# A sliding-window copy kernel: one more staged batch, larger packets, direct copies in long strided DMAs, fewer semaphore updates

## The chip, the cores and the metric

The kernel runs on one core of a Trainium2 chip. The metric is the device time in microseconds (us) of one execution; medians of several runs are quoted. Ratios are computed as the mean time of one kernel's fast runs over the mean time of the other's fast runs of the same rounds, so they are not quite the ratio of the quoted medians.

"KB" is 1024 bytes and "GB" is 10^9 bytes. A *block* is 32 KB, half a window of one batch. A DMA is cut into *packets*; the trace records start, duration, queue and size of each packet, but not which of the 16 DMA engines moved it.

## The reference

```python
batch, length, dim = (32, 4096, 256)       # float32
window_size, stride = 64, 32
n_windows = (length - window_size) // stride + 1        # 127
result = np.zeros((batch, n_windows, window_size, dim), dtype=np.float32)
for i in range(n_windows):
    start = i * stride
    result[:, i] = x[:, start:start + window_size].copy()
```

This is pure copying. A batch has 128 blocks of input. Window i consists of blocks i and i+1, so a batch has 254 blocks of output: nearly every input block is written twice.

## The kernel before

There are two ways to make the output, and the kernel uses both at once:

- *Direct* batches go from memory to memory: 254 blocks through the DMA engines, each of them both read from and written to memory (HBM).
- *Staged* batches are loaded into SBUF (128 blocks, read once) and stored from there twice, as first halves and as second halves. A store always takes all 128 rows, so it moves 256 blocks. The two surplus blocks fall on a neighbour's window and are overwritten later by an "edge" copy, which waits for the store. A staged batch costs the engines 384 blocks, but it reads memory for 128 of them only.

So staging costs DMA bytes and saves memory traffic: of the 220.95 MB that the profile below counts as read from memory, 174.8 are direct (edges included) and 46.1 loaded; of the 267.09 MB written, the same 174.8 are direct and 92.3 stored.

Three queues are used: SP issues direct copies (q1 in the profile), ACT issues loads and stores (q10), GpSimd issues the edges (q0) near the end.

```python
DIRECT, IN, OUT = 32768, 16384, 16384        # packet sizes in bytes

    def windows(self, q, b, w0, n, half=None, piece=DIRECT):
        blk = self.blk
        row = [1, 2 * blk if half is None else blk]
        h = half or 0
        return q.dma_start(
            out=self.oap((b * self.nw + w0) * 2 + h, [[2 * blk, n], row]),
            in_=self.xap(b * self.nb + w0 + h, [[blk, n], row]),
            max_dma_last_dim=piece,          # a longer row is cut into pieces of this size
        )
# ... cut ...
    staged = [*range(1, B, 3)]               # 11 of 32 batches
# ... cut ...
    edges = [(b, 0 if b - 1 in staged else 112, 15) for b in direct[:-1]]    # 15 windows each
# ... cut: a direct copy is 16 whole windows (32 packets + 16 semaphore packets),
#     or two copies of 16 half windows, more of the latter while the staged queue loads ...
        ring_r.wait_ge(near, 16)             # the edges start when the direct copies are nearly over
        for b, w, n in edges:
            for k in (b - 1, b + 1):
                if k in place and b != last:
                    st.wait_stored(ring_r, place[k])
            count(c.windows(ring_r, b, w, n), rest)
```

## Time and profile before

The median is 754.37 us of 6 runs (752.63 to 756.47).

The page of the profile, kernel before: the span; the DMA busy share and the GB/s in 40 equal slices; all packets; the direct queue q1 and the staged queue q10 with packets, MB and share of the 16 engines' span; memory traffic.

```profile
span 749.4 us, 322 instructions
...
DMA  8999999999999999999999999999999999999996
GB/s 360 401 427 429 427 429 428 434 423 418 420 424 423 418 424 415 422 427 427 414 427 417 429 432 429 430 422 430 429 423 421 423 421 419 425 426 423 431 409 262
DMA packets 18290, 313.26 MB, mean 418 GB/s; under 512 B 4336, under 2 KB 4336, under 8 KB 4528
...
q1 hardware_dynamic: 8016, 154.32, 48.8%
q10 hardware_dynamic: 9104, 138.41, 44.0%
...
HBM read 220.95 MB, written 267.09 MB: 651 GB/s over the span
...
```

The engines are 0.9 busy or more in every slice but the first and the last, so there is no gap to close. The time is bytes times the time of a packet, plus a start and an end. The packet records of the same trace, with the sum of each queue's packet times divided by 16 engines:

| kernel before | packets | size | mean ns | commonest ns | sum / 16, us |
|---|---|---|---|---|---|
| q1, direct | 4704 | 32 KB | 1236 | 1213 | 363.3 |
| q10, staged | 8448 | 16 KB | 624 | 611 | 329.6 |
| q0, edges | 608 | 32 KB | 1248 | 1213 | 47.4 |
| semaphore packets | 4336 | 4 B | 9 | 9 | 2.4 |

All packets of the three queues sum to 744.6 us. If every packet took the commonest time of its size (1213, 611, and for other sizes in the same way), the sum would be 729.5 us; I call that the *floor* and the rest, 15.1 us, the *excess*. 32 KB in 1213 ns on 16 engines is 432 GB/s.

### The profile page before, as it was taken

How to read it: one execution, taken by the hardware profiler on the slowest of the kernel's cores; microseconds unless marked ns; L12 is line 12 of the kernel's file. 1: busy time of each engine (PE TensorE's matmuls, PEld its weight loads, DVE VectorE, ACT ScalarE, POOL GpSimd, SP SyncE). 2: the span in 40 equal slices, each digit the busy share in tenths (PEclk: the TensorE clock that was granted, in tenths of full speed). 3: DMA queues.
4: the chain of work that ended last, by engine and by line, in shares of the span. 5: the costliest groups of instructions: out<-in, count | busy, mean ns of one | idle time of the engine just before them, and what ended most of it. 6: DMA issues, size and time to landing. Idle time of an engine off the chain costs nothing.

```text
span 749.4 us, 322 instructions
## 1 busy us (share of the span) xinstructions
POOL 12.8 (2%) x26
## 2 busy tenths in 40 slices
POOL 0000000000000000000000000000000000040100
DMA  8999999999999999999999999999999999999996
GB/s 360 401 427 429 427 429 428 434 423 418 420 424 423 418 424 415 422 427 427 414 427 417 429 432 429 430 422 430 429 423 421 423 421 419 425 426 423 431 409 262
DMA packets 18290, 313.26 MB, mean 418 GB/s; under 512 B 4336, under 2 KB 4336, under 8 KB 4528
## 3 DMA queue, kind: packets, MB, share of 16 engines
q1 hardware_dynamic: 8016, 154.32, 48.8%
q10 hardware_dynamic: 9104, 138.41, 44.0%
q0 software_dynamic: 1168, 20.51, 6.5%
q14 instruction: 2, 0.02, 0.0%
HBM read 220.95 MB, written 267.09 MB: 651 GB/s over the span
## 4 chain that ended last, share of the span: by engine, by line
another core or an unknown queue 92%; POOL 2%; issue 0%; POOLq 0%; SPq 0%
POOL out_dram L34 2%; POOL out_dram L44 0%; POOLq L236 0%; SPq L172 0%; POOLq L114 0%
## 5 line engine op out<-in xcount | busy, mean ns | idle before, releaser
L34 POOL DMA_DIRECT2D out_dram<-in_x_dram x21 | 12.0, 576 | 691.3 <-DMA out_dram<-in_x_dram 654.0
L44 POOL DMA_DIRECT2D out_dram<-in_x_dram x1 | 0.6, 581 | 0.0
L222 POOL MEMSET const-float32-0.0<- 128x1 f32 x1 | 0.1, 98 | 0.2 <-issue 0.2
L222 POOL MEMSET const-bfloat16-1.0<- 128x1 bf16 x1 | 0.1, 101 | 0.0
L222 POOL MEMSET const-float32-1.0<- 128x1 f32 x1 | 0.1, 98 | 0.0
L222 POOL MEMSET const-uint8-127<- 128x1 uint8 x1 | 0.1, 98 | 0.0
## 6 DMA issues: line engine op xcount, KB each, us to landing
out_dram<-in_x_dram SPq DMA_DIRECT2D x92, 1024.0 KB, 100.7
out_dram<-xb ACTq DMA_DIRECT2D x21, 4096.0 KB, 139.7
out_dram<-in_x_dram SPq DMA_DIRECT2D x110, 512.0 KB, 90.3
xb<-in_x_dram ACTq DMA_DIRECT2D x10, 4096.0 KB, 131.4
out_dram<-in_x_dram POOLq DMA_DIRECT2D x20, 960.0 KB, 38.5
xb<-in_x_dram ACTq DMA_DIRECT2D x4, 1024.0 KB, 15.7
out_dram<-xb ACTq DMA_DIRECT2D x2, 1024.0 KB, 113.4
out_dram<-xb ACTq DMA_DIRECT2D x4, 512.0 KB, 96.9
```

What stands on the lines that cost most here:

```text
L34: return q.dma_start(out=self.oap((b * self.nw + w0) * 2 + h, [[2 * blk, n], row]), in_=self.xap(b * self.nb + w0 + h, [[blk, n], row]), m ...
L44: return q.dma_start(out=self.oap((b * self.nw + w0) * 2, [[part, 16], [2 * self.blk, n], row]), in_=self.xap(b * self.nb + w0, [[part, 16 ...
L222: nc = _bacc.Bacc("TRN2", target_bir_lowering=False, num_devices=1)
```

## The change

Its intent, as the diff shows it: 12 staged batches in place of 11; 32 KB packets for loads and stores, 64 KB for edges; direct copies always half windows, 112 packets in one DMA in a pattern of 16 neighbouring rows by 7; few DMAs and so few semaphore packets (16 for each DMA of q1 and q10: 3264 for 204 DMAs on q1 before); staged loads and stores in interleaved parts (every second or fourth row), meant, I take it, to give both big queues like shares of the turns.

```diff
-DIRECT, IN, OUT = 32768, 16384, 16384
+DIRECT, IN, OUT, REST = 32768, 32768, 32768, 65536
+    def many(self, q, b, w0, n, half):
+        return q.dma_start(
+            out=self.oap((b * self.nw + w0) * 2 + half, [[2 * self.blk, 16], [32 * self.blk, n], [1, self.blk]]),
+            in_=self.xap(b * self.nb + w0 + half, [[self.blk, 16], [16 * self.blk, n], [1, self.blk]]),
+        )
 ... loads: one DMA of 128 rows -> two of 64 interleaved rows (four for the first batch);
     stores: each half in two such parts, or four for second halves of odd batches ...
-    staged = [*range(1, B, 3)]
+    staged = [0, 3, 6, 9, 11, 14, 17, 20, 22, 25, 28, 31]
 ... batch 0 may now be staged; a direct batch between two staged ones gets edges of 8 and 7 windows ...
-        for i, (b, w) in enumerate(sixteens):
-            ... cut: whole or half windows by a running share ...
+        for i, (b, w, n, half) in enumerate(main):
+            count(c.many(ring_d, b, w, n, half), near if i == len(main) - 1 else done)
 ...
-            count(c.windows(ring_r, b, w, n), rest)
+            count(c.windows(ring_r, b, w, n, None, REST), rest)
```

More of the change, by code (lines that the diff above doesn't have):

```diff
@@ L87, in load, with split @@
         i = g % len(self.tiles)
-        b, c, n = self.items[g]
         if self.count[self.stored[i]]:
             q.wait_ge(self.stored[i], self.count[self.stored[i]])
-        step = 128 // n
-        parts = [(k, 4, 32, 1) for k in range(4)] if g == 0 else [(0, step, n, step)]
-        for rows in parts:
-            self.issue(self.c.load(q, self.tiles[i], b, c, rows), self.loaded[i])
+        for rows in self.split(4 if g == 0 else 2):
+            self.issue(self.c.load(q, self.tiles[i], *self.items[g], rows), self.loaded[i])
         self.after_load[g] = self.count[self.loaded[i]]
+    def split(self, parts):
+        return [(k, parts, 128 // parts, 1) for k in range(parts)]
     def store(self, q, g):
         i = g % len(self.tiles)
-        b, c, n = self.items[g]
         q.wait_ge(self.loaded[i], self.after_load[g])
-        step = 128 // n
-        parts, end = [((0, step, n, step), 0), ((0, step, n, step), 1)], []
+        parts = [(rows, half) for half in (0, 1) for rows in self.split((2, 4 if g % 2 else 2)[half])]
+        end = []
         if g == len(self.items) - 1:
-            parts = [((0, 1, 128, 1), 1), ((0, 1, 32, 1), 0)]
+            parts = [(rows, 1) for rows in self.split((2, 4 if g % 2 else 2)[1])] + [((0, 1, 32, 1), 0)]
             end = [(96, 1, 32, 1)] + [(32 + k, 4, 16, 1) for k in range(4)]
         for rows, half in parts:
-            self.issue(self.c.store(q, self.tiles[i], b, c, rows, half), self.stored[i])
+            self.issue(self.c.store(q, self.tiles[i], *self.items[g], rows, half), self.stored[i])
         for rows in end:
-            self.issue(self.c.store(q, self.tiles[i], b, c, rows, 0), self.ended)
+            self.issue(self.c.store(q, self.tiles[i], *self.items[g], rows, 0), self.ended)
         self.after_store[g] = self.count[self.stored[i]]
@@ L140 @@
     c = Copier(x, out, B, L, D, W, S, n_win)
-    staged = [*range(1, B, 3)]
-    items = [(b, -1 if b == B - 1 else 0, c.nb) for b in staged]
-    place = {b: g for g, (b, _, n) in enumerate(items) if n == c.nb}
+    staged = [0, 3, 6, 9, 11, 14, 17, 20, 22, 25, 28, 31]
+    items = [(b, 1 if b == 0 else -1 if b == B - 1 else 0) for b in staged]
+    place = {b: g for g, b in enumerate(staged)}
     direct = [b for b in range(B) if b not in staged]
@@ L157, in count @@
         total[sem] += 16
-    sixteens = []
+    main, edges, singles = [], [], [(B - 1, c.nw - 1, 1)]
+    if 0 in staged:
+        singles.append((0, 0, 0))
+    last = B - 2
     for b in direct:
-        w = 15 if b - 1 in staged else 0
-        sixteens += [(b, w + 16 * j) for j in range((c.nw - w) // 16)]
-    singles = [(B - 1, c.nw - 1, 1)]
-    edges = [(b, 0 if b - 1 in staged else 112, 15) for b in direct[:-1]]
-    last = B - 2
-    edges.append((last, 112, 4))
-    first_loads, loads, stores = 6 * 17, 5 * 17, 6 * 34
-    turns = share = 0
+        before, behind = b - 1 in staged, b + 1 in staged
+        w = 15 if before and (not behind or b == last) else 8 if before else 0
+        if b == last:
+            w = 0
+        main += [(b, w + 16 * j, min(7, 7 - j), half) for j in range(0, 7, 7) for half in (0, 1)]
+        if b == last:
+            edges.append((b, 112, 4))
+        elif before and behind:
+            edges += [(b, 0, 8), (b, 120, 7)]
+        else:
+            edges.append((b, 0 if before else 112, 15))
     with tc.tile_critical():
         st.run(ring_s)
-        for i, (b, w) in enumerate(sixteens):
-            sem = near if i == len(sixteens) - 2 else done
-            second = turns - first_loads - stores
-            loading = turns < first_loads or 0 <= second < loads
-            share += 120 if turns < 16 or -8 <= second < 16 else 90 if loading else 18
-            if share >= 120:
-                share -= 120
-                turns += 4
-                count(c.windows(ring_d, b, w, 16, 0), done)
-                count(c.windows(ring_d, b, w, 16, 1), sem)
-            else:
-                turns += 3
-                count(c.windows(ring_d, b, w, 16), sem)
-            if i == len(sixteens) // 2:
+        for i, (b, w, n, half) in enumerate(main):
+            count(c.many(ring_d, b, w, n, half), near if i == len(main) - 1 else done)
+            if i == len(main) // 2:
                 for b, w, half in singles:
```

## The prediction

> **What bounds it now.** The 16 DMA engines. The page's slices show DMA 0.9 busy from the second to the last but one; no other engine matters. The trace's packet records, summed and divided by 16: queue q1 (direct copies) 4704 packets of 32 KB, mean 1236 ns, 363 us; q10 (staged) 8448 of 16 KB, 624 ns, 330 us; q0 (edges) 608 of 32 KB, 1248 ns, 47 us; 4336 semaphore packets of 9 ns, 2.4 us; the rest 2 us. That is 744.8 us of the 749.4 us span: no gap to close but some 6 us before the first packet and a ragged tail of some 3 us. Time = bytes x ns per packet.
>
> The commonest packet takes 1213 ns for 32 KB, 611 ns for 16 KB: 432 and 429 GB/s over 16 engines. [...] only 2% of excess over the floor is left.
>
> Where the excess sits: while the staged queue loads (about 60-150 and 440-530 us) 32 KB packets take 1213-1218 ns; while it stores, 1240-1260. In the store stretches direct copies of whole windows took 1230-1260, the half-window copies among them about 1216-1241.
>
> **What the change does, in blocks of 32 KB.**
> - One more staged batch: 128 loaded + 256 stored blocks, against 254 for a direct one. 9690 blocks in place of 9560, 317.5 MB in place of 313.3: +130 x 77 ns (1236/16) = +10 us.
> - Staged packets of 32 KB: 1213 against 2 x 611 ns, over 4224 blocks: -2.4 us. Edge packets of 64 KB: under -0.5 us.
> - About 2500 semaphore packets in place of 4336: -1 us.
> - All direct copies now half windows at 16 neighbouring rows: if they keep the half-window rate in the store stretches (about 1224 instead of 1244 ns), q1 and partly q10 gain 1 to 1.5%: -5 to -9 us. This is the uncertain term, and I take it as the real intent.
> - Turns: the records show the queues alternating packet by packet[...]. With 32 KB on both, q1 (about 324 turns) should end 54 turns before q10 (about 378); the edges fill the rest. Tail granularity rises: up to +1 us.
>
> All of it is critical, as the DMA engines never idle. Sum: q10 4608 x 1228/16 = 354; q1 4480 x 1224/16 = 343; edges 289 of 64 KB x 2455/16 = 44; rest 6: 747 us, against 744.8 before. With every packet at the floor 738, so about 748 measured; with today's excess kept 752, so about 762.
>
> **Predicted: 753 us**, 80% range 747 to 763. Faster by over 2%: 0.02; within 2%: 0.93; slower by over 2%: 0.05.
>
> **Right if:** DMA bytes rise to about 317 MB and mean GB/s from 418 to about 424; 32 KB packets of q1 and q10 mean 1220-1230 ns, and store stretches lose most of their excess; HBM read falls to about 217 MB, written stays about 267; half of the semaphore packets are gone; q1 ends around 640-670 us, edges and q10 together.
>
> **Wrong if:** the store stretches' excess comes from the mix of writes and not from the form of the copies (760-763); [...] the queues finish unequally, leaving one in a ragged tail; or 64 KB edge packets at 15 engines leave some engines a packet later (+2 us).

Three passages are cut, as marked. None is a term of the sum, which stands whole: 354 + 343 + 44 + 6 = 747 us.

## More of the kernel before

The chips differ: the kernel before took 752 to 754 us on some and 745 to 746 us on others. Kernels are therefore compared only inside one call (one chip), through their ratio to the kernel before.

The end, by stretches, kernel before (from:to in us from the span's start, length, GpSimd's busy time, clock, DMA busy share, GB/s):

```profile
core 0: us, POOL busy (x), PEclk, DMA share, GB/s
680.00:700.00 20.00, 0.00 (x0) 1.00 1.00 418
...
710.00:720.00 10.00, 0.00 (x0) 1.00 1.03 423
720.00:730.00 10.00, 0.00 (x0) 1.00 0.99 411
730.00:740.00 10.00, 0.00 (x0) 1.00 1.00 405
740.00:750.00 10.00, 0.00 (x0) 1.00 0.28 114
...
```

The share stays near 1.00 until 740 us (it can pass 1: recorded packets of one engine overlap by 3 or 4 ns, as experiment 1 reads them, and a packet is counted whole in the stretch in which it starts); only the last 10 us (0.28) drain. The packet records give 15 or 16 engines busy until 4 us before the last packet ends.

## The result

The changed kernel took 763.82 us (median of 6 runs, 762.63 to 766.12) against 754.37 us: ratio 1.0129, 95% interval 1.0107 to 1.0152. It is correct. It is slower by 1.3%, just above the predicted range of 747 to 763 us.

The same lines of the page, kernel after:

```profile
span 764.3 us, 215 instructions
...
DMA  8999999999999999999999999999999999999982
GB/s 360 430 413 418 432 427 432 430 432 432 417 425 432 422 430 418 436 425 430 410 424 434 436 424 429 433 425 432 420 427 422 429 424 432 442 412 437 396 366 120
DMA packets 12145, 317.54 MB, mean 415 GB/s; under 512 B 2559, under 2 KB 2559, under 8 KB 2767
...
q10 hardware_dynamic: 6048, 151.00, 46.6%
q1 hardware_dynamic: 5232, 147.00, 45.2%
...
HBM read 216.86 MB, written 267.19 MB: 633 GB/s over the span
...
```

DMA bytes rose from 313.26 to 317.54 MB and memory reads fell from 220.95 to 216.86 MB, as predicted; the packets fell from 18290 to 12145. But the last slices show 396, 366 and 120 GB/s where the kernel before had 431, 409 and 262. (This profile fell on the slowest of the six runs, so its span overstates the loss: 14.9 us against 9.5 between the medians.)

The end, by stretches, kernel after (same columns):

```profile
core 0: us, POOL busy (x), PEclk, DMA share, GB/s
680.00:700.00 20.00, 0.00 (x0) 1.00 1.00 421
...
710.00:720.00 10.00, 2.11 (x4) 1.00 0.94 397
720.00:730.00 10.00, 0.00 (x0) 1.00 0.98 377
730.00:740.00 10.00, 0.00 (x0) 1.00 0.95 406
740.00:750.00 10.00, 0.00 (x0) 1.00 0.68 288
750.00:760.00 10.00, 0.00 (x0) 1.00 0.24 103
...
```

In place of one draining stretch there are two, at 0.68 and 0.24, and the share is below 1 from 710 us on. The packet records say why: the last 3 us stretch in which all 16 engines worked throughout (at least 15.9 on average) ended 50 us before the last packet (4 us in the kernel before); then about 15 worked, and 8 or fewer in the last 12 us. Of the 11.8 us of idle engine time in the last 60 us (the mean over the 16 engines), 10.0 lie in the last 18 us: one idle engine is the smaller part of the loss. The records also show never more than 15 edge packets in flight at once; before the change it was 16.

To weigh the parts, both kernels were later profiled unaltered on one chip (the control runs of experiment 5). "Idle" is the time from the first to the last data packet less the busy sum; a little below zero means that the recorded packet times overlap slightly. Floors and excesses are good to about 0.2 us.

| us | before, first chip | after, first result | before, control | after, control |
|---|---|---|---|---|
| floor of its packets | 729.5 | 735.9 | 729.5 | 735.9 |
| excess over the floor | 15.1 | 12.9 | 9.8 | 6.4 |
| busy sum | 744.6 | 748.7 | 739.4 | 742.3 |
| idle, mostly at the end | -1.2 | 9.8 | -1.1 | 6.4 |
| first to last packet | 743.4 | 758.5 | 738.3 | 748.7 |

On the control chip the change adds 10.4 us: +6.4 for its bytes and packets, -3.4 of excess, +7.5 of engines that stand idle. The control profile has the least idle time of the three that were taken of the changed kernel: 6.4 us, against 9.8 here and 10.8 in after_again (experiment 4).

### The profile page after: what moved, and what is told of

Same layout as the page of the kernel before. It is cut to its first block, busy times and chain, and to the rows that moved or that the text cites. A ratio compares the mean times of both kernels' runs of the same rounds, so it can differ in the third digit from the quotient of the medians.

```text
span 764.3 us, 215 instructions
## 1 busy us (share of the span) xinstructions
POOL 12.2 (2%) x27
## 2 busy tenths in 40 slices
DMA packets 12145, 317.54 MB, mean 415 GB/s; under 512 B 2559, under 2 KB 2559, under 8 KB 2767
## 3 DMA queue, kind: packets, MB, share of 16 engines
HBM read 216.86 MB, written 267.19 MB: 633 GB/s over the span
## 4 chain that ended last, share of the span: by engine, by line
another core or an unknown queue 92%; POOL 1%; issue 0%; POOLq 0%; SPq 0%
POOL out_dram L34 1%; POOL out_dram L51 0%; POOLq L238 0%; SPq L185 0%; POOLq L121 0%
```

## The experiments

Theory 1 after the first look was: an edge copy of 15 *uncut* rows of 64 KB works on the same 15 engines every time, and one engine gets no edge at all. In the kernel before the rows are cut in two (the records name the shape "2,15"), and all 16 take part (at most 16 edge packets in flight). The rival was that the coarser staged packets or the order of the last stores make the ragged end.

### Experiment 1: packet size and shape of the edges

All four of this experiment ran on one chip, kernel before 752.04 us.

a_rest32, the changed kernel with the edge rows cut as before:

```diff
-DIRECT, IN, OUT, REST = 32768, 32768, 32768, 65536
+DIRECT, IN, OUT, REST = 32768, 32768, 32768, 32768
```

> The changed kernel with edge packets of 32 KB again (rows of 64 KB cut in two, as before the change). Theory 1 (uncut rows put the 15 windows of an edge on a fixed 15 of the 16 DMA engines, so one engine gets no edge at all and the last engine ends late): balance returns, all 16 engines busy until some 4 us before the end, time 754 to 757 us. Rival 2 (the ragged tail comes from the coarser staged packets or the order of the last stores): stays at 762 to 765 us.

Measured: 763.06 us, ratio 1.0144 (1.0121 to 1.0167). The time fell in the rival's range and not in theory 1's, yet the balance came back as theory 1 said: sixteen edge packets were in flight again and all engines worked until 10 us before the end, so the idle time fell to 3.8 us. But now the busy sum was 752.5 us: the edges took 1333 ns a packet in place of 1248.

```profile
core 0: us, POOL busy (x), PEclk, DMA share, GB/s
...
730.00:740.00 10.00, 0.00 (x0) 1.00 0.99 343
740.00:750.00 10.00, 0.00 (x0) 1.00 0.94 329
...
```

These are the last stretches of a_rest32: the engines are busy (0.99, 0.94) but move only 343 and 329 GB/s. In these traces the queues take turns packet by packet, and a turn lasts as long as its packet: at its commonest 9 ns for a semaphore packet, 611 for 16 KB, 1213 for 32 KB, 2418 for 64 KB. (The records do not name engines, but a packet starts 3 or 4 ns before another ends in 16712 of the 16740 clear links of the first trace of the kernel before. I take such a pair as following each other on one engine, so that most packets can be linked into 16 chains. In the control trace of the changed kernel, from 200 to 660 us, 3270 of 3271 clear links between two data packets go from one queue to the other.) So edges of 32 KB get a smaller share beside the staged queue's 32 KB packets than edges of 64 KB did: 175 against 212 GB/s from 690 to 720 us of the two traces. The staged queue ended 14 us before the edges, and direct copies alone run slowly (1561 ns a packet in experiment 3). Cutting the rows mended the engines' balance and broke the queues' balance. The rival was right in part: the size of the staged packets matters, through the turns.

b_rest64, the kernel before with only this part of the change:

```diff
-            count(c.windows(ring_r, b, w, n), rest)
+            count(c.windows(ring_r, b, w, n, None, 65536), rest)
```

> The kernel before with edge packets of 64 KB and nothing else changed. Theory 1: one engine runs out some 40 us early, the time rises by 7 to 11 us to 761 to 766 us. Rival 2: within 2 us of 755.

Measured: 757.72 us, ratio 1.0088 (1.0049 to 1.0126). That is 5.7 us, a little under what theory 1 expected and clearly more than its rival. At most 15 edge packets were in flight, and the last stretch with all 16 engines ended 52 us before the end. So this part of the change costs 0.9% by itself. What of that is the engine left out is not separated, as the run also changes the packet size and with it the turns: its idle time is 1.4 us (-1.2 in the first profile of the kernel before, on another chip), while its excess is 18.3 us (15.1 there).

a_half15, the changed kernel with each edge as two copies of 15 half windows, so packets of 32 KB in rows that need no cut:

```diff
-            count(c.windows(ring_r, b, w, n, None, REST), rest)
+            for half in (0, 1):
+                count(c.windows(ring_r, b, w, n, half), rest)
```

> The changed kernel with each edge issued as two copies of half windows, 15 rows of 32 KB each, so packets are 32 KB but each copy's pattern still has 15 uncut rows. If the uncut pattern of 15 rows decides which engines work (theory 1): one engine without edges, 762 to 766 us. If the 64 KB size of the packets makes the tail (rival 3): about 755 us.

Measured: 771.79 us, ratio 1.0261 (1.0236 to 1.0286), slower than either expected. At most 15 edge packets were in flight and 16 engines worked together last 39 us before the end. So it is the pattern of 15 uncut rows and not the 64 KB packet that leaves an engine out. The extra loss fits the cause of a_rest32: the staged queue ended 29 us before the last packet.

The chains of packets (see a_rest32) show how the edges lie. In after_again (the changed kernel unaltered, experiment 4) the 289 edge packets are spread over the chains like this: none on one, 17 on six or seven (one or two links are unclear), 19 to 21 on four or five, 22 on four. My reading of these counts, as the records name no engines: every uncut copy starts on the same engine and puts one row on each of the next. Then the 17 copies of 15 windows leave out one engine, and the five shorter copies (8, 7, 8, 7 and 4 windows) all load the first eight again, which gives none on one, 17 on seven, 19 on one, 21 on three, 22 on four. In the kernel before, every chain has 37 to 39 of the 608.

a_s11, the changed kernel with cut edge rows and 11 staged batches:

```diff
+DIRECT, IN, OUT, REST = 32768, 32768, 32768, 32768
-    staged = [0, 3, 6, 9, 11, 14, 17, 20, 22, 25, 28, 31]
+    staged = [*range(1, B, 3)]
```

> The changed kernel with 32 KB edge packets and the 11 staged batches of before. Bytes fall by 130 blocks of 32 KB, which at 77 ns a block is 10 us: with the tail balanced, and if the packet time stays near 1233 ns, 745 to 749 us. If fewer staged batches slow the packets (more HBM traffic, more direct copies), or if the direct queue now outlasts the staged one, 750 to 756 us.

Measured: 759.87 us, ratio 1.0101 (1.0081 to 1.0121): outside both expected ranges. Direct and staged packets were as hoped (1227 and 1231 ns), but both queues had ended 63 us before the last packet, and the edges, alone, took 1578 ns a packet.

### Experiment 2: letting the queues end together

One chip, kernel before 745.29 us. The edges wait for the semaphore `near`; an earlier direct copy can carry it.

a_early, the changed kernel with cut edge rows and

```diff
-            count(c.many(ring_d, b, w, n, half), near if i == len(main) - 1 else done)
+            count(c.many(ring_d, b, w, n, half), near if i == len(main) - 3 else done)
```

> The changed kernel with 32 KB edge packets and the edges released by the third last direct copy in place of the last. Theory 4 (in the changed kernel uncut 64 KB edge rows leave one engine without edges; cut to 32 KB they lose their larger share of the turns, so the edges outlast the staged queue and end alone, slowly): with both mended the edges and the staged queue end within 5 us of each other, edge packets mean about 1240 ns in place of 1333, and the time is 755 to 759 us, that is the cost of the added bytes alone. If the tail had another cause: 762 to 764 us.

Measured: 758.29 us, ratio 1.0149 (1.0117 to 1.0182). The queues did end within 2 us of each other, and edge packets came down to 1266 ns. The expected time was written for a chip on which the kernel before takes 752 us; against the ratio it was a miss: 1.0149 is 11 us above the kernel before, not 3 to 7, which is the size of its other range (10 to 12 us, "another cause"). With the idle time down to 3.3 us most of the loss stayed.

s11_early, as a_s11 but with `len(main) - 8`:

> The changed kernel with the 11 staged batches of before, 32 KB edge packets, edges released by the eighth last direct copy so that all three queues end together. Busy time from the packet means of the run with 11 staged batches (1227 and 1231 ns, edges at 1240 in place of 1578): 736 to 738 us in place of 749, so 746 to 751 us. If the edges among two other queues slow them all, or the queues still end apart: 752 to 757 us.

Measured: 751.06 us, ratio 1.0068 (1.0053 to 1.0083). It is the best of the altered kernels, still slower than the kernel before on that chip. Its ranges too were written for a kernel before of 752 us; by the ratio the second one held. Two stretches of it, one with direct and staged copies, one with edges as a third queue:

```profile
core 0: us, POOL busy (x), PEclk, DMA share, GB/s
...
400.00:560.00 160.00, 0.00 (x0) 1.00 1.01 433
580.00:730.00 150.00, 7.83 (x14) 1.00 1.00 399
...
```

From 580 to 730 us two of the three queues copy from memory to memory; the engines are fully busy (1.00), yet the rate is 399 in place of 433 GB/s. Something other than the engines limits that stretch.

s10_early, 10 staged batches, edges cut and released by `len(main) - 6`:

```diff
-    staged = [0, 3, 6, 9, 11, 14, 17, 20, 22, 25, 28, 31]
+    staged = [2, 5, 8, 11, 14, 17, 20, 23, 27, 31]
-            max_dma_last_dim=OUT,
+            max_dma_last_dim=OUT // 2 if half == 0 else OUT,
```

> 10 staged batches, first half-windows stored in packets of 16 KB so that the staged queue lasts as long as the direct one, edges of 32 KB released by the sixth last direct copy. Another 130 blocks of 32 KB fewer. If the DMA engines' bytes still set the time: 738 to 745 us. If direct copies without enough staged traffic are limited by memory (the edges alone took 1578 ns a packet): packets mean 1250 ns and more, 748 to 760 us.

Measured: 754.66 us, ratio 1.0128 (1.0105 to 1.0151). Direct packets took 1262 ns on average, 16 KB staged ones 653. The second expectation held: moving fewer bytes through the engines did not help.

### Experiment 3: form of the direct copies, or mix of the traffic

The prediction had seen that half-window copies ran nearer the floor than whole windows, and credited the form. The rival theory: memory has a ceiling of its own for bytes read plus bytes written. A direct block counts twice there, a staged block once, so the *direct share* of the traffic decides.

b_half, the kernel before with every direct copy as two half-window copies (ran with experiment 2):

```diff
-            if share >= 120:
-                share -= 120
+            if True:
```

> The kernel before with every direct copy issued as two half-window copies. If the form of the copy makes the excess in the store stretches (the prediction's term): 32 KB packets of the direct queue there at about 1225 ns, their mean about 1224 in place of 1236, and 3 to 6 us less busy time; the extra semaphore packets shift turns to the staged queue, so the time may not fall with it. If the mix of writes makes it: the mean stays at 1233 to 1240 ns.

Measured: 759.31 us, ratio 1.0182 (1.0169 to 1.0195). Before the end its packets were at the floor (1214 and 611 ns from 400 to 650 us), then it lost everything at the end. In the second stretch below only edges run:

```profile
core 0: us, POOL busy (x), PEclk, DMA share, GB/s
...
400.00:600.00 200.00, 0.00 (x0) 1.00 1.01 431
...
695.00:750.00 55.00, 6.32 (x12) 1.00 0.99 330
...
```

Direct copies alone: 330 GB/s with the engines busy (0.99), 1561 ns a packet. That is 660 GB/s of reads plus writes.

But b_half did not separate the theories: with 16 semaphore packets to every 16 data packets, direct copies also got fewer turns (51% of the bytes in place of 57%). The next two do. Both ran on one chip, kernel before 745.44 us. b_full has whole windows only, 32 packets and 16 semaphore packets a DMA:

```diff
-            ... the choice by share ...
+            count(c.windows(ring_d, b, w, 16), near if i == len(sixteens) - 2 else done)
```

> The kernel before with every direct copy of whole windows (two packets and a semaphore packet), so the direct queue has the large share of the turns all the time. Both theories of the excess expect 32 KB packets at 1235 to 1260 ns all along, loads too; it is the control for the next run.

b_pairs has half windows, but two 16-row groups in a DMA, so the same 32 packets and 16 semaphore packets (`many` is the changed kernel's helper):

```diff
+            j = i % 7
+            if j == 6:
+                count(c.windows(ring_d, b, w, 16), sem)
+            else:
+                count(c.many(ring_d, b, w - 16 * (j % 2), 2, j % 2), sem)
```

> The kernel before with six of seven direct copies as half windows, two 16-row groups in each, so again two packets and a semaphore packet: the same share of turns as the control, but the form of half windows. If the form makes the excess (the prediction): packets near the floor, mean about 1220 ns. If the mix makes it (direct copies read and write memory, staged transfers only do one; read plus written memory traffic near 660 GB/s is a second ceiling): 1235 to 1260 ns as in the control, within 5 ns of it.

Measured: b_full 758.48 us, ratio 1.0172 (1.0157 to 1.0188); b_pairs 756.97 us, ratio 1.0157 (1.0140 to 1.0173). The direct packets took 1242 and 1244 ns over the whole run: no difference. The same stretch of each, b_full first:

```profile
core 0: us, POOL busy (x), PEclk, DMA share, GB/s
200.00:400.00 200.00, 0.00 (x0) 1.00 1.00 424
...
```

```profile
core 0: us, POOL busy (x), PEclk, DMA share, GB/s
200.00:400.00 200.00, 0.00 (x0) 1.00 1.01 423
...
```

424 and 423 GB/s: at an equal share of turns (0.58) the form makes no difference here. The packet records of several runs, put in order of the direct share, show the two ceilings. Times in this table count from the trace's start, 7 us before the span's. "Read + written" is worked out as twice the direct rate plus the staged rate:

| stretch | direct share | DMA GB/s | read + written GB/s | 32 KB direct packet, ns |
|---|---|---|---|---|
| b_half, 400-650 us | 0.51 | 431 | 653 | 1214 |
| after, control, 400-640 us | 0.53 | 432 | 660 | 1216 |
| after, first chip, 400-640 us | 0.53 | 428 | 653 | 1229 |
| before, first chip, 160-420 us | 0.57 | 422 | 663 | 1245 |
| b_full / b_pairs, 200-420 us | 0.58 | 423 | 670 | 1241 / 1242 |
| s11_early, 595-740 us | 0.67 | 400 | 666 | 1310 |
| b_half, edges alone, 705-755 us | 1.00 | 334 | 668 | 1566 |

At direct shares of 0.51 to 0.53, in b_half and on the control chip, the rate is 431 and 432 GB/s, that of packets at the floor; the highest in any stretch of 80 us or more that was asked for is 433 (s11_early). I take this as the engines' limit. The page has 432 for the changed kernel of the control pair and 425 for the kernel before, before_again first, then after_again2:

```profile
core 0: us, POOL busy (x), PEclk, DMA share, GB/s
140.00:400.00 260.00, 0.00 (x0) 1.00 1.00 425
...
```

```profile
core 0: us, POOL busy (x), PEclk, DMA share, GB/s
...
400.00:640.00 240.00, 0.00 (x0) 1.00 1.00 432
...
```

Above that share, the sum of reads and writes stays at 663 to 670 GB/s in these stretches (655 to 672 in others of the kept traces) while the DMA rate falls by more than a fifth. Staged packets slow down as well (16 KB ones from 611 ns in the first row to 625 in the fourth, 32 KB ones from 1214 in the second to 1319 in s11_early), so it is not a cost of the direct packets alone. That the limit lies in the memory is inferred from the sum; and on the first chip the changed kernel stayed under both limits (428 and 653), which they do not explain. The most that one core reached in the table, reading and writing together, is 670 GB/s.

### Experiment 4: mending the tail by other means

a_even (same chip as b_full) is the changed kernel with cut edge rows, and with the first half windows of the last two staged batches and the final rows stored in 16 KB packets, so that the staged queue keeps turns until the edges are done:

```diff
+DIRECT, IN, OUT, REST = 32768, 32768, 32768, 32768
+        late = g >= len(self.items) - 2
+            piece = OUT // 2 if late and half == 0 else OUT
+            self.issue(self.c.store(..., rows, half, piece), self.stored[i])
```

> The changed kernel with 32 KB edge packets, and the first half windows of the last two staged batches stored in 16 KB packets, so that the staged queue has more turns left and should end with the edges. If the tail is the whole cause of what the change lost beside the bytes: the last 60 us have under 4 us of idle engine time (11.9 in the changed kernel), the time is 0.5 to 1.2% under the changed kernel of this call and within 0.6% of the kernel before. If not: over 1.0% above the kernel before.

> The changed kernel unaltered, so that it stands beside the others on the same chip: 1.2 to 1.5% above the kernel before, with one engine out of work some 40 us before the end as in the first run.

Measured: the unaltered changed kernel (after_again) 759.26 us, ratio 1.0178 (1.0154 to 1.0201), more than the 1.2 to 1.5% expected; a_even 755.06 us, ratio 1.0141 (1.0116 to 1.0167). The ratio of a_even lies in its "if not" range, while the gain over the changed kernel, 0.55% by the medians, lies at the low end of the other; by the ratios it is under 0.4% and their intervals overlap, so it is not clear of the noise. By the measure of the expectation, idle engine time in the last 60 us fell from 13.0 to 4.0 us (between first and last packet, from 10.8 to 1.8), but the busy sum rose from 742.9 to 747.0 us: edges at 1281 ns, late 16 KB stores at 650. So half of what was mended came back as slower packets, and the tail is only part of the loss. From 680 to 720 us a_even reached neither ceiling (409 GB/s through the engines, 593 read plus written); why its last stores were slow there is not settled.

### Experiment 5: bytes or forms, on one chip

By now both theories of the tail had been tested and 12 batches still lost. One chip, kernel before 745.88 us. Two runs are unaltered controls:

> The kernel before, unaltered, for a profile on the same chip as the others of this call. Chips differ by 1% (752 to 754 us and 745 us so far). On a chip where it takes 745 us I expect the direct queue's packets at about 1223 ns and the staged at about 617, busy time about 737 us, as its bytes were the same and only the excess can be smaller.

> The changed kernel, unaltered, for a profile on the same chip as the one before. The difference of busy time should be what the 130 added blocks cost at the floor (130 x 1213/16 ns = 9.9 us) less 3 to 4 us for larger packets and fewer semaphores, so 5 to 7 us more; and idle engine time at the end 9 to 11 us more.

Measured: before_again gave 1227 and 619 ns for q1 and q10 and a busy sum of 739.4 us. after_again2 took 757.87 us, ratio 1.0164 (1.0139 to 1.0190). Busy time rose by 2.9 us in place of the expected 5 to 7, because the excess fell as well; idle time rose by 7.5 us in place of 9 to 11. Lines of the page, first before_again, then after_again2:

```profile
span 744.3 us, 322 instructions
...
DMA packets 18290, 313.26 MB, mean 421 GB/s; under 512 B 4336, under 2 KB 4336, under 8 KB 4528
...
HBM read 220.95 MB, written 267.09 MB: 656 GB/s over the span
...
```

```profile
span 754.5 us, 215 instructions
...
DMA packets 12145, 317.54 MB, mean 421 GB/s; under 512 B 2559, under 2 KB 2559, under 8 KB 2767
...
HBM read 216.86 MB, written 267.19 MB: 642 GB/s over the span
...
```

The kernel before keeps memory at 656 GB/s over the whole span, close to the 663 to 670 of the table; the changed kernel at 642. It was given slack at the memory by taking more of the engines, and both pages show the same 421 GB/s through the engines over the span.

s12_forms is the changed kernel with all its forms undone and only the twelfth batch and the constant half-window share kept:

```diff
-DIRECT, IN, OUT, REST = 32768, 32768, 32768, 65536
+DIRECT, IN, OUT, REST = 32768, 16384, 16384, 32768
 ... loads and stores whole again (split(1)) ...
-            count(c.many(ring_d, b, w, n, half), near if i == len(main) - 1 else done)
+            count(c.windows(ring_d, b, w, 16, half), near if i == len(main) - 1 else done)
```

> 12 staged batches as in the change, but all else as before it: staged packets of 16 KB in whole loads and stores, direct copies as single half-window copies of 16 rows, edge packets of 32 KB. Direct share about 52% of the bytes and a balanced tail. If the added bytes alone are the lasting cost: packets at the floor (1214 to 1222 ns, 611 to 618 ns), idle time at the end under 5 us, time 0.3 to 1.2% over the kernel before. If twelve staged batches are better as such and only the new forms lost: at or under the kernel before.

Measured: 758.60 us, ratio 1.0165 (1.0148 to 1.0182), the same as the changed kernel. Its packets were at the floor to 680 us (1214 and 611 ns), better than the changed kernel's, but its edges outlasted the staged queue by 17 us and took 1368 ns. The expectation about the packets held; the one about the tail and both ranges of the time did not, so its time does not price the bytes alone. Nor does it acquit the new forms, as one tail took the place of another; it shows only that undoing them did not make twelve batches faster.

No version beat the kernel before. The floor of twelve batches' packets in the changed form (735.9 us) is only 2.4 us under what the kernel before needs from its first to its last packet on the control chip (738.3 us), so a twelfth batch could gain at most that, with no excess and no idle engine.

## Why the prediction was wrong

The predicted time was 753 us, range 747 to 763; measured were 763.82. That the times would lie within 2% of each other was right; in place of a gain of 1 us came a loss of 9.5.

- **Bytes, packets, semaphores.** Right. 9690 blocks were predicted and 317.54 MB moved; memory read 216.86 and written 267.19 MB. Semaphore packets fell from 4336 to 2559, worth 1.0 us at 9 ns. Floor to floor these terms come to +6.4 us; the prediction's +10, -2.4, -0.5 and -1 sum to +6. But the mean rate fell from 418 to 415 GB/s where about 424 was predicted, and the 32 KB packets took 1232 (q1) and 1235 ns (q10) where it said 1220 to 1230.
- **"All direct copies now half windows ... -5 to -9 us".** The mechanism was wrong and the size too large. The excess fell by 2.2 us on the first chip and by 3.4 us on the control chip. The form is not the cause: b_pairs and b_full ran alike, while b_half and b_pairs, both of half windows, ran at 1214 and 1242 ns with direct shares of 0.51 and 0.58. In the changed kernel the share went from 0.57 to 0.53 in the store stretches. The prediction read a correlation inside one trace (half-window copies are the ones that also take fewer turns) as a cause. Its own list of what could be wrong named the mix of writes; it was the mix, though of reads and writes together. That list put 760 to 763 us beside it, close to the 763.82; this is luck, as the excess did fall and the loss lay at the end.
- **The busy sum.** Nearly right: 747 predicted, 748.7 measured on the first chip.
- **"Tail granularity rises: up to +1 us" and "64 KB edge packets at 15 engines ... (+2 us)".** This is the step that failed. It let some engines end one packet later, up to 3 us in all; idle time rose by 11.0 us in the first pair of profiles and by 7.5 us in the control pair. By the chains of after_again, as read in experiment 1, the uncut copies use the same first engines: four chains get 22 edge packets of 64 KB where an even spread gives 18.1 (289 over 16). These 3.9 packets of 2.45 us are 9.7 us, an estimate from the traces' own numbers that lies between the two measured. The engine left out is the smaller part: 17 copies at 2.4 us are 41 us of one engine, which is 2.6 us over 16. The larger part, by that reading, is that all five shorter edges fall on the same eight engines; b_rest64, with one such edge in place of five, has 3.1 us of idle time in its last 18 us where the changed kernel has 10.0. No run changed the shorter edges alone. With uncut edges alone b_rest64 lost 0.9%; with cut edges a_rest32 had 3.8 us of idle time in place of 9.8, but lost it again through the turns.
- **From busy time to time.** A slip of arithmetic. The kernel before has 744.6 us busy and a median of 754.4, about 10 us more (its profiled run was a quick one, 751.2). The prediction added these 10 us to its two bounds (738 to 748, 752 to 762) but only 6 to its best sum of 747. Done alike, it would have said 757.
- **"The edges fill the rest".** The queues ended together as planned (768.8 and 770.0 us in the trace), but the engines within them did not.

What stays open: the part of the remaining loss that belongs to the twelfth batch as such. a_even, with its idle time mended to 1.8 us, was still 1.4% slower than the kernel before, but its tail had slow stores that reached neither ceiling. An estimate from the table is +6.4 us of floor less 3.4 us of excess, 3 us or 0.4%; no run shows it cleanly.

## What to carry to other kernels

This copy kernel had two ceilings, bytes through the DMA engines (432 GB/s) and bytes read plus written at memory (663 to 670 GB/s), and moving a batch from one to the other added 6.4 us of floor at the engines for 3.4 us less excess. Look for both in your own traces, and price a staged block and a direct block against both, stretch by stretch, before adding either. When busy time hardly changes and the time does, count how many engines work in the last 50 us: here copies of 15 uncut rows had at most 15 packets in flight and left one chain of after_again without edges, and the shorter ones brought four chains to 22 packets where others had 17. Changing a packet size also changed the queue's share of turns (175 GB/s for edges of 32 KB against 212 for 64 KB) and with it which queue was left alone at the end. A difference between two forms inside one trace is a cause only after a run holds everything else equal, the share of turns first.
